# A two-layer hybrid attention block: balanced column halves, later row scaling, a later gate transposition, and one gated product behind a weight split

## The chip, the cores and the metric

The kernel runs on one core of a Trainium2 chip. The metric is device time in microseconds (us) from launch to end, the median of several runs of the same program. Beside it there is one profiled execution, whose trace says when each instruction ran on each engine: PE is TensorE (matmuls; PEld are its weight loads), DVE is VectorE, ACT is ScalarE, POOL is GpSimd, SP is the engine whose queue issues all DMAs here.

## The reference, cut to what matters

512 latent tokens `x` and 256 context tokens `ctx`, model width 1024, go through two layers. Everything is float32.

```python
for i in range(2):
    mod_x = silu(c) @ w_ada[i] + b_ada[i]            # six rows of 1024: sh1, sc1, g1, sh2, sc2, g2
    mod_c = silu(c_ctx) @ w_ada[i] + b_ada[i]        # the same for the context
    hx, hc = x * (1 + sc1) + sh1, ctx * (1 + csc1) + csh1
    # layer 0: windowed attention, 16 heads of 64; layer 1: differential attention, 8 pairs of heads
    ax, ac = mixer_i(hx, hc)                         # with its output projection
    x = layer_norm(alpha * x + g1 * ax)
    x = layer_norm(alpha * x + g2 * (square(relu((x * (1 + sc2) + sh2) @ w1[i])) @ w2[i]))
    if i == 0:                                       # the context takes part in layer 0's MLP too
        ctx = layer_norm(alpha * ctx + cg1 * ac)
        ctx = layer_norm(alpha * ctx + cg2 * mlp(ctx))
return x
```

So layer 0 works on 768 tokens, layer 1's queries and MLP on 512. Layer 1's attention takes, for each of 8 heads, two softmaxes over 768 keys, and subtracts one from the other.

## The kernel before, in words

**Products in three parts.** Each float32 operand is split into a rounded high part (`w_h`, made by ACT as a cast) and the rest (`w_l`, made by DVE as a subtraction). `mm3` issues high*high, high*low and low*high, so each product is three matmuls (lines 318, 319, 320). `wsplit` issues the DMA of a weight piece into `w_raw`, the cast and the subtraction. There are three `w_raw` buffers (a fourth later) and four pairs `w_h`, `w_l`, so a DMA waits until DVE has finished with an older piece.

**Order of work.** PE's order is fixed by a planner in the program (`Flow`): jobs are Python generators that yield a condition, and the planner goes on with the first job whose condition holds in its own model of time. The orders of the other engines are made from it by the scheduler of the framework; each engine then works through its own queue in order, waiting on semaphores. `tc.add_manual_dep(..., ORDER)` puts one instruction behind another in a queue without a wait; `behind(fn, ins)` adds a real wait on another engine's instruction.

**MLP of layer 0** (`mlp` with `ntok` = 768). Four chunks of 1024 hidden units. In a chunk, for each of eight groups `ft` of 128 hidden units, `h_ps` (two banks of PSUM, 1024 columns) takes 24 matmuls over the first 512 tokens and 24 over the other 256 (in chunk 0 the first two groups go in slices of 256). ACT reads it with a relu, DVE or POOL squares, ACT and DVE split into `hid`. Then `y_ps` products with `hid` follow. In chunks 0 to 3 DVE also works off `ada_rows`: dot products that give `mods`, the modulation rows still missing, from transposed weights (`w_raw<-in_w_adaT`, two or four DVE operations a row block). When such a row is complete, `ada_gate` transposes it on PE (`gate_t`), ACT copies it (`gate_s`), SP stores it (`gate_d`), and it is later loaded again as a row over all partitions. Row (0, 5), layer 0's second gate, is used in chunk 2.

**Layer 1's attention.** For each head `proj1` computes `qkv_ps` for six token blocks; `post1` rotates and splits the result, and PE transposes it (`kT_ps` from `sk`, `qT_ps` from `sq`). `scores1` makes `s_ps` (queries by 768 keys) with two matmuls of 512 columns and two of 256, then DVE takes the minimum `nm` and ACT the exponential. Beside it `resid1` prepares the residual of the output in 16 steps on POOL: `rs_x * rs_g + rs_b`. Each fourth step loads new `rs_g` and `rs_b` by DMA, and DVE scales them by `alpha`; that scaling stands where the load is issued.

**Layer 1's output projection** (`tok_product` and `gated_add`). For each token block and half, PE ends a sum `y_ps` whose first parts were made earlier; DVE multiplies by the gate row `g1x` (`g_tmp`), adds into `acc`, and takes statistics. The last weight piece, `b_wo[1, 3]`, is loaded at the start of this stage; `xn_t` are the transpositions after the normalisation, `hx_v`, `hx1m` their results.

Of the kernel before, what the change touches and what calls it, by code (L numbers as in the profile page):

```python
# [216 lines left out]
def pool2(n):  # L217
    return n * 0.0022 + 0.12
# [16 lines left out]
def hybrid_block(ctx: ExitStack, tc: tile.TileContext, t: dict, out: bass.AP):  # L235
# [63 lines left out]
    def wsplit(src, n=1024, raw=None, hl=None, pool=False):  # L299
        if raw is None:  # L300
            raw = raw_tile()
        if hl is None:
            hl = [wpool.tile([P, 1024], F32R, name="w_" + x, tag="w" + x, bufs=NH) for x in "hl"] + [rwh.get(), rwh]
        raw, rg, rr = raw
        h, l, hg, hr = hl
        q = dma(n, [rg], out=raw[:, :n], in_=src)
        a = ac(n, [q, hg], nc.scalar.copy, out=h[:, :n], in_=raw[:, :n])
        kw = dict(out=l[:, :n], in0=raw[:, :n], in1=f(h)[:, :n], op=ALU.subtract)
        d = gp(pool2(n), [a], nc.gpsimd.tensor_tensor, **kw) if pool else dv(n, [a], nc.vector.tensor_tensor, **kw)
        d.ring = rr  # L310
        rel = Task()
        rel.ring = hr
        return Weight(h, l, d, rel)
# [128 lines left out]

    def ada_gate(l, m, dep):
        gd = dram.tile([2 - l, KT, P], F32, name=f"gate_d{l}{m}")
        yield from to_rows(mods[l][:, m] if l == 0 else mods[l][:, m, :, 0], gd, dep)
        gate_d[(l, m)] = gd.rearrange("s k p -> s (k p)")

# [106 lines left out]
    def gated_add(pool, give, acc, half, pt, p, gate, last, scale=1.0):  # L554
        cs_ = slice(half * 512, (half + 1) * 512)
        tm = pool.tile([P, 512], F32, name="g_tmp", tag="tmp", bufs=2)
        m = dv(512, [p], nc.vector.tensor_tensor, out=tm, in0=pt, in1=gate[:, cs_], op=ALU.mult)
        give(m)
        if scale != 1.0:
            return dv(512, [m], nc.vector.scalar_tensor_tensor, out=acc[:, cs_], in0=acc[:, cs_], scalar=scale, in1=tm,  # L560
                      op0=ALU.mult, op1=ALU.add)
        if last:
            return dv(512, [m], nc.vector.tensor_tensor, out=acc[:, cs_], in0=acc[:, cs_], in1=tm, op=ALU.add)
        return gp(pool2(512), [m], nc.gpsimd.tensor_tensor, out=acc[:, cs_], in0=acc[:, cs_], in1=tm, op=ALU.add)
# [76 lines left out]
    def mlp(l, hx, ready, apool, pool, ntok, acc, gates, done, extra, res, XR=0):  # L641
        ntb = ntok // P
        first = [slice(i, i + 256) for i in range(0, ntok, 256)]
        parts = [slice(0, 512)] + ([slice(512, ntok)] if ntok > 512 else [])
        fx = [pool.tile([P, D], F32, name="fx", tag="fx", bufs=ntb) for _ in range(ntb)]


# [16 lines left out]

        row_gates = gates
        for ch in range(4):
            hid = [apool.tile([P, 2, 2, ntok], F32R, name="hid", tag="A", bufs=4) for _ in range(4)]
            state = {}

            def post(ft, pt, slot, p):  # L670
                hd, fi = hid[ft // 2], ft % 2
                r = pool.tile([P, max(ntok, XR)], F32, name="relu", tag="xr", bufs=2)
                a = ac(ntok, [p], nc.scalar.activation, out=r[:, :ntok], in_=pt[:, :ntok], func=AF.Relu)
                if slot is not None:
                    sS.give(slot, a)
                if ch:
                    a = gp(pool2(ntok), [a], nc.gpsimd.tensor_tensor, out=r[:, :ntok], in0=r[:, :ntok],
                           in1=r[:, :ntok], op=ALU.mult)
                else:
                    a = dv(ntok, [a], nc.vector.tensor_tensor, out=r[:, :ntok], in0=r[:, :ntok], in1=r[:, :ntok],  # L680
                           op=ALU.mult)
                split(ntok, a, r[:, :ntok], hd[:, fi, 0], hd[:, fi, 1])

            n0 = 0 if ch else 2 if ntok > 512 else 4
            order = [(ft, sl) for sl in first for ft in range(n0)] + [(ft, sl) for ft in range(n0, 8) for sl in parts]
            for n, (ft, sl) in enumerate(order):
                if ch == 0:
                    yield lambda: [ready[b] for b in range(sl.start // P, sl.stop // P)]
                if sl.start == 0:
                    odd = n0 == 4 and ft in (1, 3)  # L690
                    if not odd:
                        yield sS.ok
                        state["ps"] = psS("h_ps"), sS.take()
                    pt, slot = state["ps"]
                    state[ft] = (wsplit(t["w1"][l, ch * 8 + ft], pool=ch == 0 and ft in WP[l]), pt[:, 512:1024] if odd else pt,
                                 None if n0 == 4 and ft in (0, 2) else slot)
                w, pt, slot = state[ft]
                yield w.t
                for k in range(KT):
                    c_ = slice(k * P, (k + 1) * P)  # L700
                    mm3(pt[:, sl], w.h[:, c_], w.l[:, c_], hxs(hx, k, 0, sl), hxs(hx, k, 1, sl), k == 0, k == KT - 1)
                    if k % 4 == 3:
                        p = fl.pe(12 * mm(sl.stop - sl.start))
                        if k == 3:
                            yield
                if sl.stop == ntok:
                    fl.finish(w.rel)
                    post(ft, pt, slot, p)
                if extra is not None and (4 < n < 16 if ch == 0 else ft < 6 and sl.start == 0):
                    next(extra, None)  # L710
                yield
            if ch == 2:
                gates = yield from row_gates()
            yield from tok_product(pool, hid, lambda half: [wsplit(t["w2"][l, ch, half, u]) for u in range(4)],
                                   [(h_, tb) for h_ in range(2) for tb in range(ntb)], acc, gates,
                                   done if ch == 3 else None, extra=extra, sink=sum_up(ch, gates) if ch < 3 else None)
# [461 lines left out]
    with tc.tile_pool(name="attn1", bufs=1, reuse_waits="tile") as pool:  # L1178
# [104 lines left out]
        def resid1():  # L1283
            def load(n):
                i, tb = n // NXB, n % NXB
                c = slice(i * 256, i * 256 + 256)
                if tb == 0:
                    gb[:] = [pool.tile([P, 256], F32, name="rs_" + n_, tag="rs_" + n_, bufs=1) for n_ in "gb"]
                    for k in range(2):
                        dma(256, [], out=gb[k], in_=lnrow[0, 2 + k:3 + k][:, c].broadcast_to([P, 256]))  # L1290
                        dv(128, [], nc.vector.tensor_scalar, out=gb[k], in0=gb[k], scalar1=ALPHA, scalar2=None,
                           op0=ALU.mult)
                x = pool.tile([P, 256], F32, name="rs_x", tag="rs_x", bufs=3)
                return x, dma(256, [], out=x, in_=x_spill[tb][:, c]), x_res[tb][:, c], list(gb)

# [2 lines left out]
            for n in range(4 * NXB):  # L1298
                after = yield
                x, q, dst, (g, b) = nxt  # L1300
                d = gp(pool2(256), [q], behind(nc.gpsimd.tensor_tensor, after), out=x, in0=x, in1=g, op=ALU.mult)
                d = gp(pool2(256), [d], nc.gpsimd.tensor_tensor, out=x, in0=x, in1=b, op=ALU.add)
                if old:
# [8 lines left out]
        def scores1(hd_, R):  # L1312
            kS, qTt = R["kS"], R["qT"]
            yield lambda: R["ready"]
            for qb in range(4):
                em = []
                for tt in range(2):
# [1 line left out]
                    ei = eS1.take()  # L1319
                    sp = psS("s_ps")  # L1320
                    slot = sS.take()
                    for c0, c1 in ((0, 512), (512, TOK)):
                        for hl in range(2):
                            nc.tensor.matmul(out=sp[:, c0:c1], lhsT=qTt[:, tt, hl, qb * P:(qb + 1) * P],  # L1324
                                             rhs=kS[:, tt, c0:c1], start=(hl == 0), stop=(hl == 1))
                    p = fl.pe(2 * mm(512) + 2 * mm(256))
                    nm = small.tile([P, 1], F32, name="nm", tag="nm")
                    d = dv(TOK, [p], nc.vector.tensor_reduce, out=nm, in_=sp[:, 0:TOK], axis=AX.X, op=ALU.min)
                    e = pool.tile([P, TOK], F32, name="e1", tag="e", bufs=EB1)
                    if tt == 0:  # L1330
                        sm = st["s0"][hd_ // NG][:, qb, hd_ % NG:hd_ % NG + 1]
                    else:
                        sm = small.tile([P, 1], F32, name="sm", tag="sm")
                    a = ac(TOK + 200, [d], nc.scalar.activation, out=e, in_=sp[:, 0:TOK], func=AF.Exp, scale=-1.0,
                           bias=nm, accum_out=sm)
                    sS.give(slot, a)
                    em.append((e, sm, ei, a))
                    yield
# [172 lines left out]
    with tc.tile_pool(name="mlp1", bufs=1, reuse_waits="tile") as pool:  # L1511
# [5 lines left out]
        gx = bcast_load(pool, gate_d[(1, 2)][0:1], "g1x")  # L1517
        queue["behind"] = queue["last"]
        st2["W1"].append(wsplit(t["b_wo"][1, 3], hl=hl + [None, None]))
        lb = bcast_load(pool, lnrow[1, 1:2], "l1b")  # L1520
        scale_inplace(lb, ALPHA)
        A, B = affine(1, 0, 1, 1, 3, 4, "m1", 1)
# [106 lines left out]
```

## Time and profile before

| | us |
|---|---|
| median of 3 runs | 1710.75 (1710.18 to 1711.88) |
| the profiled execution's own time | 1715.99 |
| span of its trace, first to last instruction | 1714.2 |

| engine | busy, us | share |
|---|---|---|
| PE | 1634.3 | 95% |
| DVE | 957.7 | 56% |
| ACT | 658.1 | 38% |
| POOL | 345.9 | 20% |

PE's mean granted clock was 0.985. A matmul's record lasts longer than its share of PE, since matmuls overlap: the pace is read from start to start. A row of the timeline gives start, length, engine, line, operation, and in brackets how long the engine had been idle and what ended that.

### The profile page before, as it was taken

The numbers are of one execution on the slowest core, as the hardware profiler recorded it, in microseconds if no ns is written. First come the engines' busy times: TensorE is split into PE (matmuls) and PEld (weight loads), VectorE is DVE, ScalarE is ACT, GpSimd is POOL, SyncE is SP. The second block draws the span as 40 slices with busy tenths as digits, with TensorE's granted clock in tenths as the row PEclk, the third lists the DMA queues.
The fourth block names the chain that finished last, engine by engine and source line by source line (L and its number), as shares of the span: only waits on it lengthen the run. The fifth ranks groups of instructions, "written<-read, shape, count | busy, mean of one in ns | idle before, by whom it ended". The sixth has DMA issues, their size and how long they took to land.

```text
span 1714.2 us, 23438 instructions
## 1 busy us (share of the span) xinstructions
PE 1634.3 (95%) x9129; PEld 1359.1 (79%) x9129; DVE 957.7 (56%) x1811; ACT 658.1 (38%) x1281; POOL 345.9 (20%) x314
## 2 busy tenths in 40 slices
PE   6899899999899999999999999999989799999998
PEld 4787567788778878878878998999877788888886
DVE  3665677676764644445346767777655553233336
ACT  3455555462212302302315555555542533223230
POOL 1233444200001201243220122220100001103422
PEclk9999999999999999999999999999999899999999
DMA  9110441243443434324222222211132214232321
GB/s 361 40 50 32 148 171 52 84 169 112 159 147 111 148 111 141 111 91 156 81 81 102 63 68 66 72 44 37 47 111 99 99 62 134 74 121 76 111 86 50
DMA packets 57240, 174.78 MB, mean 102 GB/s; under 512 B 7144, under 2 KB 13096, under 8 KB 57128
## 3 DMA queue, kind: packets, MB, share of 16 engines
q1 hardware_dynamic: 57128, 173.27, 29.9%
q8 instruction: 72, 1.18, 0.3%
q14 instruction: 40, 0.33, 0.1%
HBM read 165.35 MB, written 7.90 MB: 101 GB/s over the span
## 4 chain that ended last, share of the span: by engine, by line
PE 75%; DVE 9%; issue 5%; ACT 4%; POOL 3%; DMA 3%; SPq 0%; POOLq 0%; DVEq 0%; ACTq 0%
PE y_ps L320 10%; PE y_ps L319 10%; PE y_ps L318 10%; PE h_ps L318 8%; PE h_ps L319 8%; PE h_ps L320 8%; PE o_ps L1014 2%; PE qkv_ps L318 2%; PE s_ps L1324 2%; PE qkv_ps L319 2%; PE qkv_ps L320 2%; DVE e L260 2%; DVE w_l L260 2%; PE pT_ps L1028 2%; ACT w_h L264 1%
## 5 line engine op out<-in xcount | busy, mean ns | idle before, releaser
L264 ACT CAST w_h<-w_raw 128x1024 fp32r<-128x1024 f32 (+1 forms) x185 | 186.5, 1014 | 425.5 <-PE y_ps L320 214.1
L260 DVE TENSOR_TENSOR w_l<-w_raw,w_h 128x1024 fp32r<-128x1024 f32 (+1 forms) x185 | 221.9, 1209 | 223.5 <-ACT w_h L264 223.4
L319 PE MATMUL y_ps<-w_l,hid 128*128 128x512 f32 x640 | 253.0, 395 | 2.2 <-DVE w_l L260 2.2
L320 PE MATMUL y_ps<-w_h,hid 128*128 128x512 f32 x640 | 252.9, 395 | 0.6 <-DVE hid L260 0.6
L318 PE MATMUL y_ps<-w_h,hid 128*128 128x512 f32 x640 | 253.0, 395 | 0.0
L268 POOL TENSOR_TENSOR relu<-relu 128x768 f32<-128x768 f32 (+1 forms) x48 | 81.5, 1697 | 613.9 <-ACT relu L264 613.9
L320 PE MATMUL h_ps<-hx0m,w_l 128*128 128x256 f32 (+1 forms) x528 | 176.2, 334 | 0.9 <-DVE w_l L260 0.9
L318 PE MATMUL h_ps<-hx0m,w_h 128*128 128x256 f32 (+1 forms) x528 | 176.7, 335 | 0.0
L319 PE MATMUL h_ps<-hx0m,w_h 128*128 128x256 f32 (+1 forms) x528 | 176.0, 333 | 0.0
L319 PEld LDWEIGHTS y_ps<-w_l,hid 128*128 128x128 f32 x640 | 120.4, 188 | 31.7 <-DVE w_l L260 3.9
L320 PEld LDWEIGHTS y_ps<-w_h,hid 128*128 128x128 f32 x640 | 120.4, 188 | 30.1 <-DVE hid L260 1.9
L318 PEld LDWEIGHTS y_ps<-w_h,hid 128*128 128x128 f32 x640 | 120.4, 188 | 28.4
L318 PE MATMUL qkv_ps<-w_h,hx 128*128 128x384 f32 (+1 forms) x384 | 128.2, 334 | 0.2
L319 PE MATMUL qkv_ps<-w_l,hx 128*128 128x384 f32 (+1 forms) x384 | 123.7, 322 | 0.8 <-DVE w_l L260 0.8
L320 PE MATMUL qkv_ps<-w_h,hx 128*128 128x384 f32 (+1 forms) x384 | 123.4, 321 | 0.0
L268 POOL TENSOR_TENSOR e<-e,sm 128x512 f32<-128x512 f32 (+2 forms) x96 | 95.4, 1010 | 127.6 <-DVE sm L260 107.1
L318 PE MATMUL h_ps<-hx1m,w_h 128*128 128x512 f32 (+1 forms) x288 | 108.1, 375 | 3.5 <-ACT relu L264 3.5
L320 PEld LDWEIGHTS h_ps<-hx0m,w_l 128*128 128x128 f32 x528 | 99.7, 189 | 12.9 <-DVE w_l L260 1.7
L318 PEld LDWEIGHTS h_ps<-hx0m,w_h 128*128 128x128 f32 x528 | 99.7, 189 | 11.4 <-ACT w_h L264 0.2
L319 PEld LDWEIGHTS h_ps<-hx0m,w_h 128*128 128x128 f32 x528 | 99.7, 189 | 11.3
L319 PE MATMUL h_ps<-hx1m,w_h 128*128 128x512 f32 (+1 forms) x288 | 107.6, 374 | 0.0
L320 PE MATMUL h_ps<-hx1m,w_l 128*128 128x512 f32 (+1 forms) x288 | 107.5, 373 | 0.0
(225 smaller groups left out, 3124.1 us busy)
## 6 DMA issues: line engine op xcount, KB each, us to landing
w_raw<-in_w SPq DMA_DIRECT2D x128, 512.0 KB, 3.5
w_raw<-in_w_adaT SPq DMA_DIRECT2D x56, 512.0 KB, 3.5
w_raw<-in_w_ada SPq DMA_DIRECT2D x24, 512.0 KB, 3.9
w_raw<-in_b_w SPq DMA_DIRECT2D x32, 384.0 KB, 3.4
raw<-in_w_ada SPq DMA_DIRECT2D x16, 512.0 KB, 9.6
w_raw<-in_a_wq SPq DMA_DIRECT2D x8, 512.0 KB, 7.1
w_raw<-in_a_wo SPq DMA_DIRECT2D x8, 512.0 KB, 3.6
w_raw<-in_b_wo SPq DMA_DIRECT2D x8, 512.0 KB, 4.4
```

The costliest lines, as they stand in the source:

```text
L260: fn(**kw)
L264: fn(**kw)
L268: fn(**kw)
L318: nc.tensor.matmul(out=o, lhsT=lh, rhs=rh, start=start, stop=False)
L319: nc.tensor.matmul(out=o, lhsT=lh, rhs=rl, start=False, stop=False)
L320: last["pe"] = nc.tensor.matmul(out=o, lhsT=ll, rhs=rh, start=False, stop=stop)
L1014: nc.tensor.matmul(out=po[odd * HD:odd * HD + HD, 0:256], lhsT=vv[:, kb, kvh], rhs=pt_[:, odd * 256:odd * 256 + 256], start=(i == 0), stop ...
L1028: nc.tensor.transpose(out=pp[:, c * P:(c + 1) * P], in_=es[j][:, i * P:(i + 1) * P], identity=ident)
L1324: nc.tensor.matmul(out=sp[:, c0:c1], lhsT=qTt[:, tt, hl, qb * P:(qb + 1) * P], rhs=kS[:, tt, c0:c1], start=(hl == 0), stop=(hl == 1))
```

## The change

Six edits, joined:

1. In layer 0's MLP the 768 tokens go in halves of 384 and 384, not 512 and 256. The second half is written at column 512 of `h_ps`, so each half lies in one bank; the relu reads the two stretches as a two-dimensional pattern.
2. The scores of layer 1 go in the same way, two matmuls of 384 columns for each half of the keys; the minimum and the exponential read the two stretches.
3. The transposition of row (0, 5) (`gate_t`) waits in the planner until chunk 1 of layer 0's MLP begins.
4. The scaling of `rs_g` and `rs_b` moves from the place of the load to the step that first uses them, with a wait on the PE transposition `kT_ps` of that step.
5. In DVE's queue the first gated product of layer 1's output projection stands behind the subtraction of the last weight piece.
6. `wsplit` and `gated_add` keep the instruction for that (no instruction of their own).

```diff
@@ wsplit @@
+            last["split"] = nc.vector.tensor_tensor(**kw)
+            d = fl.op("D", dve(n), [a])
@@ ada_gate @@
+        if (l, m) == (0, 5):
+            yield lambda: YES if "second" in st2 else NO
@@ gated_add @@
-        m = dv(512, [p], nc.vector.tensor_tensor, out=tm, in0=pt, in1=gate[:, cs_], op=ALU.mult)
+        i = nc.vector.tensor_tensor(out=tm, in0=pt, in1=gate[:, cs_], op=ALU.mult)
+        if queue.get("split"):
+            tc.add_manual_dep(i.ins, queue.pop("split"), ORDER, reason="queue order")
+        m = fl.op("D", dve(512), [p])
@@ mlp @@
-        parts = [slice(0, 512)] + ([slice(512, ntok)] if ntok > 512 else [])
+        parts = [slice(0, 512)] if ntok <= 512 else [slice(0, ntok // 2), slice(ntok // 2, ntok)]
+            if l == 0 and ch == 1:
+                st2["second"] = True
-                a = ac(ntok, [p], nc.scalar.activation, out=r[:, :ntok], in_=pt[:, :ntok], func=AF.Relu)
+                ro, ri = r[:, :ntok], pt[:, :ntok]
+                if ntok > 512 and ft >= n0:
+                    ro = ro.rearrange("p (b t) -> p b t", b=2)
+                    ri = pt.rearrange("p (b t) -> p b t", b=2)[:, :, 0:ntok // 2]
+                a = ac(ntok, [p], nc.scalar.activation, out=ro, in_=ri, func=AF.Relu)
+                    po = sl if ft < n0 or sl.start == 0 else slice(512, 512 + sl.stop - sl.start)
+                    mm3(pt[:, po], w.h[:, c_], w.l[:, c_], hxs(hx, k, 0, sl), hxs(hx, k, 1, sl), k == 0, k == KT - 1)
@@ resid1 @@
-                        dv(128, [], nc.vector.tensor_scalar, out=gb[k], in0=gb[k], scalar1=ALPHA, ...)
+                for y in (g, b) if n % NXB == 0 else ():
+                    dv(128, [], behind(nc.vector.tensor_scalar, after), out=y, in0=y, scalar1=ALPHA, ...)
@@ scores1 @@
-                    for c0, c1 in ((0, 512), (512, TOK)):
+                    for c in range(2):
                         for hl in range(2):
+                            nc.tensor.matmul(out=sp[:, c * 512:c * 512 + 384], lhsT=qTt[:, tt, hl, qb * P:(qb + 1) * P],
+                                             rhs=kS[:, tt, c * 384:c * 384 + 384], start=(hl == 0), stop=(hl == 1))
+                    sv = sp.rearrange("p (b t) -> p b t", b=2)[:, :, 0:384]
+                    d = dv(TOK, [p], nc.vector.tensor_reduce, out=nm, in_=sv, axis=AX.XY, op=ALU.min)
+                    a = ac(TOK + 200, [d], nc.scalar.activation, out=e.rearrange("p (b t) -> p b t", b=2),
+                           in_=sv, func=AF.Exp, scale=-1.0, bias=nm, accum_out=sm)
@@ before layer 1's output projection @@
         st2["W1"].append(wsplit(t["b_wo"][1, 3], hl=hl + [None, None]))
+        queue["split"] = last["split"].ins.name
```

What moves in the queues. First PE, in chunk 0 of layer 0's MLP, where `gate_t` stood between two groups of hidden units (`h_ps`, from activations `hx0m` and weights):

```order
L320 MATMUL h_ps<-hx0m,w_l 128x256
L435 MATMUL gate_t<-identr,mods_81 16x128
L318 MATMUL h_ps<-hx0m,w_h 128x512
L319 MATMUL h_ps<-hx0m,w_h 128x512
L320 MATMUL h_ps<-hx0m,w_l 128x512
```

Now it stands 384 matmuls later, behind the last product of chunk 0 (`y_ps`) and ahead of the first of chunk 1:

```order
L324 MATMUL y_ps<-w_h,hid 128x512
L439 MATMUL gate_t<-identr,mods_81 16x128
L322 MATMUL h_ps<-hx0m,w_h 128x384
L323 MATMUL h_ps<-hx0m,w_h 128x384
L324 MATMUL h_ps<-hx0m,w_l 128x384
```

On SP the store of that row moves with it, behind 22 more weight loads, and the two loads of the row behind eight more; in DVE's queue some dot products of `ada_rows` go behind `w_l` subtractions, and none is added.

Second DVE, in layer 1's attention, at the end of a head (the two last blocks of a head are context tokens, whose `sk` is split straight from `qkv_ps`; `rms_sb` belongs to the head before). Before:

```order
L260 TENSOR_TENSOR vt_8449<-qkv_ps,vt_8449 128x128
L260 TENSOR_SCALAR rs_g<-rs_g 128x256
L260 COPY rms_sb<-rms_ps 128x128
L260 TENSOR_SCALAR rs_b<-rs_b 128x256
L260 TENSOR_TENSOR sk<-qkv_ps,sk 128x2x64
L260 TENSOR_TENSOR w_l<-w_raw,w_h 128x768 x3
```

Now:

```order
L260 TENSOR_TENSOR vt_8449<-qkv_ps,vt_8449 128x128
L260 COPY rms_sb<-rms_ps 128x128
L260 TENSOR_TENSOR sk<-qkv_ps,sk 128x2x64
L312 TENSOR_TENSOR w_l<-w_raw,w_h 128x768 x3
```

The two scalings left this place; they stand in the next head behind two minima `nm`. The same happens in the heads after it, four times in all. In the third of these heads the planner also interleaves PE's `pT_ps`, `o_ps`, `kT_ps`, `qT_ps` and `qkv_ps` in another order; the rest of PE's order is as before.

Third DVE, at the start of layer 1's output projection. Before:

```order
L260 TENSOR_TENSOR oT_8245<-oraw,oT_8245 128x512 x2
L260 TENSOR_TENSOR g_tmp<-y_ps,g1x 128x512
L260 TENSOR_TENSOR acc_12405<-acc_12405,g_tmp 128x512
L260 BN_STATS bn<-acc_12405 128x6
L260 TENSOR_TENSOR w_l<-w_raw,w_h 128x1024
L260 TENSOR_SCALAR l1b<-l1b 128x1024
L260 TENSOR_TENSOR g_tmp<-y_ps,g1x 128x512
```

Now:

```order
L260 TENSOR_TENSOR oT_8245<-oraw,oT_8245 128x512 x2
L312 TENSOR_TENSOR w_l<-w_raw,w_h 128x1024
L260 TENSOR_SCALAR l1b<-l1b 128x1024
L563 TENSOR_TENSOR g_tmp<-y_ps,g1x 128x512
L260 TENSOR_TENSOR acc_12405<-acc_12405,g_tmp 128x512
L260 BN_STATS bn<-acc_12405 128x6
L563 TENSOR_TENSOR g_tmp<-y_ps,g1x 128x512
```

The subtraction and the scaling of `l1b` moved ahead of three instructions.

More of the change, by code (lines that the diff above doesn't have):

```diff
@@ L308, in wsplit @@
         kw = dict(out=l[:, :n], in0=raw[:, :n], in1=f(h)[:, :n], op=ALU.subtract)
-        d = gp(pool2(n), [a], nc.gpsimd.tensor_tensor, **kw) if pool else dv(n, [a], nc.vector.tensor_tensor, **kw)
+        if pool:
+            d = gp(pool2(n), [a], nc.gpsimd.tensor_tensor, **kw)
+        else:
+            last["split"] = nc.vector.tensor_tensor(**kw)
+            d = fl.op("D", dve(n), [a])
         d.ring = rr
@@ L700, in mlp @@
                     c_ = slice(k * P, (k + 1) * P)
-                    mm3(pt[:, sl], w.h[:, c_], w.l[:, c_], hxs(hx, k, 0, sl), hxs(hx, k, 1, sl), k == 0, k == KT - 1)
+                    po = sl if ft < n0 or sl.start == 0 else slice(512, 512 + sl.stop - sl.start)
+                    mm3(pt[:, po], w.h[:, c_], w.l[:, c_], hxs(hx, k, 0, sl), hxs(hx, k, 1, sl), k == 0, k == KT - 1)
                     if k % 4 == 3:
@@ L1290, in load @@
                         dma(256, [], out=gb[k], in_=lnrow[0, 2 + k:3 + k][:, c].broadcast_to([P, 256]))
-                        dv(128, [], nc.vector.tensor_scalar, out=gb[k], in0=gb[k], scalar1=ALPHA, scalar2=None,
-                           op0=ALU.mult)
                 x = pool.tile([P, 256], F32, name="rs_x", tag="rs_x", bufs=3)
@@ L1300, in resid1 @@
                 x, q, dst, (g, b) = nxt
+                for y in (g, b) if n % NXB == 0 else ():
+                    dv(128, [], behind(nc.vector.tensor_scalar, after), out=y, in0=y, scalar1=ALPHA, scalar2=None,
+                       op0=ALU.mult)
                 d = gp(pool2(256), [q], behind(nc.gpsimd.tensor_tensor, after), out=x, in0=x, in1=g, op=ALU.mult)
@@ L1321, in scores1 @@
                     slot = sS.take()
-                    for c0, c1 in ((0, 512), (512, TOK)):
+                    for c in range(2):
                         for hl in range(2):
-                            nc.tensor.matmul(out=sp[:, c0:c1], lhsT=qTt[:, tt, hl, qb * P:(qb + 1) * P],
-                                             rhs=kS[:, tt, c0:c1], start=(hl == 0), stop=(hl == 1))
-                    p = fl.pe(2 * mm(512) + 2 * mm(256))
+                            nc.tensor.matmul(out=sp[:, c * 512:c * 512 + 384], lhsT=qTt[:, tt, hl, qb * P:(qb + 1) * P],
+                                             rhs=kS[:, tt, c * 384:c * 384 + 384], start=(hl == 0), stop=(hl == 1))
+                    sv = sp.rearrange("p (b t) -> p b t", b=2)[:, :, 0:384]
+                    p = fl.pe(4 * mm(384))
                     nm = small.tile([P, 1], F32, name="nm", tag="nm")
-                    d = dv(TOK, [p], nc.vector.tensor_reduce, out=nm, in_=sp[:, 0:TOK], axis=AX.X, op=ALU.min)
+                    d = dv(TOK, [p], nc.vector.tensor_reduce, out=nm, in_=sv, axis=AX.XY, op=ALU.min)
                     e = pool.tile([P, TOK], F32, name="e1", tag="e", bufs=EB1)
@@ L1333, in scores1 @@
                         sm = small.tile([P, 1], F32, name="sm", tag="sm")
-                    a = ac(TOK + 200, [d], nc.scalar.activation, out=e, in_=sp[:, 0:TOK], func=AF.Exp, scale=-1.0,
-                           bias=nm, accum_out=sm)
+                    a = ac(TOK + 200, [d], nc.scalar.activation, out=e.rearrange("p (b t) -> p b t", b=2),
+                           in_=sv, func=AF.Exp, scale=-1.0, bias=nm, accum_out=sm)
                     sS.give(slot, a)
```

## The prediction, as put on record before the run

> **What bounds the kernel now.** I read the page first: which engine is busy.
>
> ```profile
> PE 1634.3 (95%) x9129; PEld 1359.1 (79%) x9129; DVE 957.7 (56%) x1811; ACT 658.1 (38%) x1281; POOL 345.9 (20%) x314
> ```
>
> PE bounds the kernel. A change can take time out of its pace or out of its waits. So next I read whom PE waits for, longest first (total, times, longest):
>
> ```profile
> PE kT_ps L1229 <- DVE sk L260: 8.5, 6, 2.3
> ...
> PE y_ps L319 <- DVE w_l L260: 5.3, 5, 3.1
> ...
> PE gate_t L435 <- DVE mods L260: 4.9, 1, 4.9
> ```
>
> Three of the longest are places that the diff touches: DVE's queue at the ends of heads, the last weight piece, and the transposition of the gate row. The granted clock (the number after the five engines; instructions in brackets) says what stands behind each wait:
>
> ```profile
> 433.90:438.80 4.90, 4.89 (x12) 3.87 (x13) 3.56 (x5) 1.30 (x2) 0.00 (x0) 0.50 0.66 213
> 1001.60:1005.40 3.80, 3.79 (x18) 3.80 (x19) 2.76 (x4) 1.56 (x4) 0.00 (x0) 0.55 0.64 205
> 1310.40:1313.70 3.30, 0.18 (x1) 0.00 (x0) 3.23 (x5) 0.00 (x0) 0.00 (x0) 0.83 0.00 0
> 1313.70:1319.40 5.70, 5.70 (x13) 4.46 (x14) 2.54 (x4) 0.00 (x0) 0.00 (x0) 0.50 0.77 265
> ```
>
> After each of the three waits PE runs at half clock for some microseconds, and in the third row the clock falls inside the wait. So a wait costs more than its idle time.
>
> **A. The gate transposition** (edit 3). PE's and DVE's rows:
>
> ```profile
> 428.78 0.28 PE L320 MATMUL h_ps<-hx0m,w_l 128*128 128x256 f32 x1
> 433.91 0.38 PE L435 MATMUL gate_t<-identr,mods 128*16 128x128 f32 x1 [4.85 <-DVE mods L260]
> 434.01 0.76 PE L318 MATMUL h_ps<-hx0m,w_h 128*128 128x512 f32 x1
> 439.06 0.40 PE L318 MATMUL h_ps<-hx0m,w_h 128*128 128x512 f32 x1
> 428.51 1.23 DVE L260 TENSOR_TENSOR w_l<-w_raw,w_h 128x1024 fp32r<-128x1024 f32 x1 [1.28 <-ACT w_h L264]
> 437.56 1.23 DVE L260 TENSOR_TENSOR w_l<-w_raw,w_h 128x1024 fp32r<-128x1024 f32 x1 [1.29 <-ACT w_h L264]
> ```
>
> The idle time is 4.85. From 434.01 to 439.06 twelve matmuls of 512 columns took 5.05; at 0.233 each (below) they take 2.80, so half clock cost 2.25. Together 7.1. The transposition itself stays, with operands long ready. What is late next is `w_l`: without the wait PE would want the first of the two pieces at 428.9 + 0.47 (it serves the third matmul) and have it at 429.74, and the second (8.4 later) at about 438.2, to have it at 438.79. That is 0.4 + 0.6 = 1.0 which the stall hid. A = 6.1, between 4.5 (PE also waits in the new place, by a wait like the 1.03 under C, and a little more) and 7.1 (`w_l` comes earlier).
>
> The store and the loads of the row now stand ahead of weight loads on SP. At 520.3, where chunk 0's products end, those loads have several pieces of lead; I cost this at nothing, and it is a rival below.
>
> **B. First end of a head** (edit 4). Here DVE waits for two DMAs ahead of `sk` (the first row is the page's, with the median time to landing):
>
> ```profile
> w_raw<-in_b_w SPq DMA_DIRECT2D x32, 384.0 KB, 3.4
> 1001.61 0.33 PE L1229 MATMUL kT_ps<-identr,sk 128*128 128x128 f32 x2 [2.31 <-DVE sk L260]
> 999.56 0.29 DVE L260 TENSOR_SCALAR rs_g<-rs_g 128x256 f32<-128x256 f32 x1 [1.60 <-DMA rs_g<-in_lnrow]
> 1000.97 0.29 DVE L260 TENSOR_SCALAR rs_b<-rs_b 128x256 f32<-128x256 f32 x1 [0.92 <-DMA rs_b<-in_lnrow]
> 1002.36 7.32 SPq L275 DMA_DIRECT2D w_raw<-in_b_w  x4
> 1008.36 0.96 DVE L260 TENSOR_TENSOR w_l<-w_raw,w_h 128x768 fp32r<-128x768 f32 x1 [2.46 <-ACT w_h L264]
> 1009.54 0.34 PE L318 MATMUL qkv_ps<-w_h,hx 128*128 128x384 f32 x1
> ```
>
> Without the two waits PE gains 2.3, and the half clock behind them (1001.60 to 1005.40 at 0.55: 3.8 x 0.45 = 1.7): 4.0. But the head's fourth weight piece then ends last: its DMA goes out at 1002.36, DVE ends its split at 1009.32, and PE wants it at 1009.54, now 4.0 earlier. The DMA waits in SP's queue behind loads of `rs_x` until about 1001.6, so the chain gains 0.75 at least, and PE 0.9 with the 0.2 that it had to spare. The transfer took some 5 here (to the cast of 0.87 ahead of 1008.36), against 3.4 at the median; with that, 1.7 more, at most 2.8. I take 2.0, nearer to the usual transfer.
>
> **C. Second and third ends.** The second end against the fourth, where nothing is loaded any more for `rs_x` (rows of 1124.09 and 1128.88):
>
> ```profile
> 1039.89 0.43 PE L1420 MATMUL rms_ps<-osq,c_selT 128*32 128x128 f32 x8
> 1046.32 0.60 PE L1449 MATMUL rmsB<-identr,rr 128*2 128x128 f32 x4 [0.54 <-POOL rr L268]
> 1124.09 0.43 PE L1420 MATMUL rms_ps<-osq,c_selT 128*32 128x128 f32 x8
> 1128.88 0.60 PE L1449 MATMUL rmsB<-identr,rr 128*2 128x128 f32 x4 [1.03 <-POOL rr L268]
> 1083.90 0.29 DVE L260 TENSOR_SCALAR rs_g<-rs_g 128x256 f32<-128x256 f32 x1 [3.69 <-DMA rs_g<-in_lnrow]
> ```
>
> 6.43 against 4.79: the scalings cost 1.6 there, and POOL's `rr` ends last in both. The third DVE wait, 3.69, is the longest, but PE's six waits for `sk` were 8.5 together and at most 2.3, and the largest of them were elsewhere: it is hidden but for some tenths, and I take 0.2. C = 1.8, between 1.0 and 2.2. In their new places the scalings stand behind minima that end after `kT_ps` in all four heads, so I cost their added waits at nothing; if one came early, DVE would hold the next exponential's input for some tenths. PE's new order in the third head: 0, between 1.0 lost and 1.0 gained, as waits in the ends of heads are of that size.
>
> **D. The gated product behind the last split** (edit 5).
>
> ```profile
> 1301.93 1.04 ACT L264 CAST w_h<-w_raw 128x1024 fp32r<-128x1024 f32 x1
> 1310.38 0.69 DVE L260 TENSOR_TENSOR g_tmp<-y_ps,g1x 128x512 f32<-128x512 f32 x1 [7.63 <-PE y_ps L320]
> 1312.44 1.21 DVE L260 TENSOR_TENSOR w_l<-w_raw,w_h 128x1024 fp32r<-128x1024 f32 x1
> 1310.18 0.40 PE L318 MATMUL y_ps<-w_h,oT 128*128 128x512 f32 x1
> 1313.70 0.80 PE L319 MATMUL y_ps<-w_l,oT 128*128 128x512 f32 x1 [3.13 <-DVE w_l L260]
> 1318.80 0.69 DVE L260 TENSOR_TENSOR g_tmp<-y_ps,g1x 128x512 f32<-128x512 f32 x1 [1.14 <-PE y_ps L320]
> 1330.33 0.69 DVE L260 TENSOR_TENSOR g_tmp<-y_ps,g1x 128x512 f32<-128x512 f32 x1 [0.30 <-PE y_ps L320]
> ```
>
> The piece was ready at 1302.97, and DVE sat idle 7.63 in front of the gated product, with the split behind it. Now the split runs in that idle time. PE alone gains 3.52 - 0.23 (1310.18 to 1313.70, less one matmul) and, over the 13 matmuls to 1319.40 (the last clock row), 5.70 - 3.03 = 2.7: 6.0. Then DVE ends last: from 1318.80 on it was busy until 0.30 before 1330.33, 11.2 for the third to the eighth gated product. With its first products back to back (two steps of 0.7 each behind 1312.4) the third starts at 1313.9 and the eighth at 1325.1, 5.2 earlier, when PE has just ended its part. The normalisation, `xn_t` and the MLP follow that. D = 5.2, between 3.3 (the clock falls anyway) and 6.0.
>
> [...]
>
> **E. Halves of 384** (edits 1, 2).
>
> ```profile
> 402.01 0.39 PE L318 MATMUL h_ps<-hx0m,w_h 128*128 128x512 f32 x1
> 407.60 0.28 PE L318 MATMUL h_ps<-hx0m,w_h 128*128 128x256 f32 x1
> 399.20 0.28 PE L318 MATMUL h_ps<-hx0m,w_h 128*128 128x256 f32 x1
> 970.04 0.34 PE L318 MATMUL qkv_ps<-w_h,hx 128*128 128x384 f32 x1
> 973.18 0.40 PE L1324 MATMUL s_ps<-kS,qT 128*128 128x512 f32 x1
> ```
>
> 24 matmuls of 512 columns (402.01 to 407.60) take 5.59, 0.233 each; 24 of 256 (399.20 to 402.01) take 2.81, 0.117 each; 18 of 384 take 3.14, 0.174 each. A group costs 8.40 now and 48 x 0.1744 = 8.37 then. 6 groups in chunk 0 and 24 in the others: 0.9 gained. The scores: 64 times 0.003, 0.2. The relu reads as many columns as before, in two stretches, beside matmuls. E = 1.1; as some runs of 384 go by 0.002 slower than this one, the lower end is -2.4.
>
> **The sum.** 6.1 + 2.0 + 1.8 + 5.2 + 1.1 = 16.2. The profiled execution took 1715.99, with 1.8 around its span; it would take 1699.8. It lies 5.2 above the median of the runs, 1710.75; the terms are waits which these runs have too, so I take them from the median: 1694.5.
>
> **Rivals.**
> 1. The half-clock stretches stay, since they come with these stages and not with these waits. Against it speaks that in all three places the clock fell at the wait. Only idle time goes: 4.85 - 1.0 in A, 0.9 in B, 1.8 in C, 3.3 in D, 1.1 in E: 11, so 1700. Chance 0.12. [...]
> 2. SP's queue: the moved store waits for ACT's copy, the load behind it for the store, and weight pieces of chunk 1 for both. One late piece costs a DMA's way and a stretch of half clock, as in A, 7: the gain shrinks to 9, 1702. Against it: PE reaches that point 6 earlier while the weights are several pieces ahead. Chance 0.07.
> 3. Slower: a matmul of 384 columns over `hx0m` into `h_ps` costs more than over `hx` into `qkv_ps`, since the row that I price it by streams weights, not activations. There are 30 x 48 = 1440 of them. The other terms gain 15.3; from 0.185 each the kernel is no faster, from 0.187 it is slower by over 0.2%. At 0.233, the price of a whole bank, it would be 1780. Nothing in the profile speaks for it; chance 0.03.
> 4. PE's waits move instead of going (the next weight piece, POOL's `rr`, DVE's normalisation), and what is left can't be told from no change, 0.2% being about what a measurement of this kernel can tell: 1709. Chance 0.04.
>
> **Numbers.** My forecast has the rest, 0.74, with a range of its own from 1689 (all upper ends: 7.1 + 2.8 + 2.2 + 6.0 + 1.1, the third head's order 1.0, and the 4.0 of B in full, together 21.4) to 1699. The whole range reaches to 1702, for rivals 1 and 2. Faster 0.93 (the forecast and rivals 1 and 2), same 0.04, slower 0.03.
>
> **What would show it.** The trace afterwards should have no wait at `gate_t`, no half clock near 430 and at the output projection, and none of the waits of DVE for `rs_g`; a short wait for `w_l` in the first head's end; 48 matmuls in 8.37. It is wrong if `h_ps` matmuls start more than 0.18 apart, if ACT waits for `in_w` early in chunk 1, or if the clock falls at new places.

## The result and the profile after

| | before | all changes |
|---|---|---|
| median, us | 1710.75 (1709.49 to 1711.88, 5 runs) | 1699.93 (1699.34 to 1701.91, 5 runs) |
| ratio | | 0.9939 [0.9925, 0.9954] |
| profiled execution, us | 1715.99, span 1714.2 | 1701.91, span 1700.1 |
| mean granted clock in it | 0.985 | 0.988 |

The kernel is faster by 10.8 us, where 16.2 were forecast; between the two profiled executions the difference is 14.1. Two more samples of the same kernel, among the experiments, gave ratios of 0.9938 and 0.9931.

The engines after the change, from the page:

```profile
PE 1629.0 (96%) x9129; PEld 1392.8 (82%) x9129; DVE 956.8 (56%) x1811; ACT 658.2 (39%) x1281; POOL 347.0 (20%) x314
```

PE is busy for 5.3 us less, and still bounds the kernel. PE's waits (total, times, longest):

```profile
PE kT_ps L1246 <- DVE sk L260: 7.9, 6, 2.3
...
PE y_ps L323 <- DVE w_l L312: 1.7, 2, 1.3
...
PE qkv_ps L323 <- DVE w_l L312: 0.8, 2, 0.6
```

The wait at `gate_t` (4.9) is gone from the list, and `y_ps` waits 1.7 for `w_l` instead of 5.3. The waits of `qkv_ps` for `w_l` are 0.8 together as before, but the longest has moved from the third head's end (1093.59) to the first's, where the prediction expected one. The waits for `sk` are hardly shorter in sum, 7.9 instead of 8.5: the 2.31 of the first head's end is gone, and one of 1.71 in the third head is new. The longest that is left, 2.32, is that of a later head, which no edit touches.

PE's timeline shows the places one after the other: the gate row's transposition, 48 matmuls of 384 columns (counted from 518.98; the 49th starts at 527.30), and the first head's end:

```profile
512.91 0.40 PE L324 MATMUL y_ps<-w_h,hid 128*128 128x512 f32 x1
513.15 0.27 PE L439 MATMUL gate_t<-identr,mods 128*16 128x128 f32 x1
513.17 0.42 PE L322 MATMUL h_ps<-hx0m,w_h 128*128 128x384 f32 x1
...
518.98 0.34 PE L322 MATMUL h_ps<-hx0m,w_h 128*128 128x384 f32 x1
...
527.30 0.34 PE L322 MATMUL h_ps<-hx0m,w_h 128*128 128x384 f32 x1
...
997.57 0.45 PE L322 MATMUL qkv_ps<-w_h,hx 128*128 128x384 f32 x1 [0.33 <-ACT w_h L264]
998.56 0.45 PE L323 MATMUL qkv_ps<-w_l,hx 128*128 128x384 f32 x1 [0.55 <-DVE w_l L312]
```

The transposition runs without a wait, and chunk 1 begins at 513.17 (before: at 520.5). The 48 matmuls take 8.32. In the first head's end the fourth weight piece now ends last, with waits of 0.33 and 0.55 in place of the 2.31 for `sk`.

In the output projection DVE's queue now has the split where it was meant to be, ahead of the idle time:

```profile
1295.30 1.22 DVE L312 TENSOR_TENSOR w_l<-w_raw,w_h 128x1024 fp32r<-128x1024 f32 x1 [0.26 <-ACT w_h L264]
1296.44 0.69 DVE L260 TENSOR_SCALAR l1b<-l1b 128x1024 f32<-128x1024 f32 x1
1302.67 0.69 DVE L563 TENSOR_TENSOR g_tmp<-y_ps,g1x 128x512 f32<-128x512 f32 x1 [5.55 <-PE y_ps L324]
```

Last, stretches of the timeline with PE's granted clock behind the five engines: the first head's end, a place in the third head, the output projection, and the end of a later head.

```profile
998.40:1002.20 3.80, 3.64 (x21) 3.63 (x22) 3.37 (x10) 2.04 (x5) 0.29 (x1) 1.00 0.34 103
1065.80:1069.20 3.40, 2.80 (x14) 2.40 (x13) 2.40 (x6) 1.44 (x3) 0.58 (x1) 0.50 0.28 81
...
1298.00:1304.00 6.00, 6.00 (x27) 4.84 (x27) 1.29 (x2) 0.00 (x0) 0.00 (x0) 1.00 0.65 245
1202.30:1212.60 10.30, 10.30 (x31) 9.02 (x31) 5.48 (x7) 4.01 (x8) 0.00 (x0) 0.50 0.32 118
```

The half clock of the first head and the one behind the split in the output projection are gone (both rows at 1.00). A stretch at 1065.8 is new (0.50), and the one near 1203, at a place that the change doesn't touch, is 10.2 long instead of 6.8. This last point turned out to matter for the whole case: the program had not changed there.

### The profile page after: what moved, and what is told of

The parts are those of the page before. It is cut to its first block, busy times and chain, and to the rows that moved or that the text cites. A ratio compares the mean times of both kernels' runs of the same rounds, so it can differ in the third digit from the quotient of the medians.

```text
span 1700.1 us, 23451 instructions
## 1 busy us (share of the span) xinstructions
PE 1629.0 (96%) x9129; PEld 1392.8 (82%) x9129; DVE 956.8 (56%) x1811; ACT 658.2 (39%) x1281; POOL 347.0 (20%) x314
## 4 chain that ended last, share of the span: by engine, by line
PE 76%; DVE 10%; ACT 4%; issue 3%; DMA 3%; POOL 3%; SPq 0%; DVEq 0%; POOLq 0%; ACTq 0%
PE y_ps L324 10%; PE y_ps L322 10%; PE y_ps L323 10%; PE h_ps L322 8%; PE h_ps L323 8%; PE h_ps L324 8%; PE o_ps L1031 2%; PE qkv_ps L322 2%; PE qkv_ps L323 2%; PE s_ps L1342 2%; PE qkv_ps L324 2%; PE pT_ps L1045 2%; DVE w_l L312 2%; DVE e L260 2%; PE o_ps L1380 1%
## 5 line engine op out<-in xcount | busy, mean ns | idle before, releaser
L312 DVE TENSOR_TENSOR w_l<-w_raw,w_h 128x1024 fp32r<-128x1024 f32 (+1 forms) x185 | 220.3, 1202 | 221.0 <-ACT w_h L264 218.6
L324 PE MATMUL h_ps<-hx0m,w_l 128*128 128x384 f32 (+1 forms) x528 | 175.4, 332 | 1.3 <-DVE w_l L312 1.3
L322 PE MATMUL h_ps<-hx0m,w_h 128*128 128x384 f32 (+1 forms) x528 | 175.4, 332 | 0.0
L323 PE MATMUL h_ps<-hx0m,w_h 128*128 128x384 f32 (+1 forms) x528 | 175.1, 332 | 0.0
```

The costliest lines, as they stand in the source:

```text
L312: last["split"] = nc.vector.tensor_tensor(**kw)
L322: nc.tensor.matmul(out=o, lhsT=lh, rhs=rh, start=start, stop=False)
L323: nc.tensor.matmul(out=o, lhsT=lh, rhs=rl, start=False, stop=False)
L324: last["pe"] = nc.tensor.matmul(out=o, lhsT=ll, rhs=rh, start=False, stop=stop)
```

## The experiments

All ran with five rounds beside the kernel before. Differences below are of medians unless they are called differences of stages in a profile. The first four had no run of all of the changes beside them; they are set against the 1699.93 above.

**The scalings' new place, the old plan.** The scalings stand where the change puts them, but the planner is told of them at the old place, so PE's order in the heads is that of before:

```diff
@@ resid1, load @@
+                        fl.op("D", dve(128), [])
@@ resid1, step @@
-                    dv(128, [], behind(nc.vector.tensor_scalar, after), out=y, in0=y, scalar1=ALPHA, ...)
+                    behind(nc.vector.tensor_scalar, after)(out=y, in0=y, scalar1=ALPHA, ...)
```

> The changed kernel, with the planner told of the two scalings at their old place (the instructions stay at the new one): PE's order in layer 1's attention is that of before. Theory 1 (the third head's new order cost 2.8 us: a wait of 1.7 for sk and half clock behind it): 1697.1 us, ratio to before 0.992, no wait over 0.5 us for sk in the third head. Rival (that wait only took the place of others; the third DMA wait of DVE, 3.69 us, was what the head had to lose): 1699.9 us, as the changed kernel, with another wait in the third head.

1699.11 us, ratio 0.9936 [0.9924, 0.9949]. By the milestones of the two profiles its third head was about 2.5 shorter, by the median the whole was not to be told from all of the changes.

**The gate back** (edit 3 undone).

```diff
-        if (l, m) == (0, 5):
-            yield lambda: YES if "second" in st2 else NO
```

> The changed kernel without the later gate transposition. Theory 1 (the stall costs its idle time and half clock behind it, in every run): 1706.5 us (6.6 more than the changed kernel), a wait of 4.9 us at gate_t and half clock behind it. Rival (in most runs the clock does not fall, so that a run loses only the idle time less 1.0): 1703.8 us (3.9 more).

1705.46, ratio 0.9975 [0.9964, 0.9986]: 5.5 slower than all of the changes (6.2 by the ratios), between the 6.6 of the first theory and the 3.9 of the rival, and near the 6.1 at which the prediction priced edit 3.

**The split back** (edit 5 undone).

```diff
-        queue["split"] = last["split"].ins.name
```

> The changed kernel without the order between the first gated product and the last split. Theory 1 (idle time and half clock, DVE last): 1705.7 us (5.8 more than the changed kernel), a wait of 3.1 us for w_l in the output projection. Rival (only the idle time counts in most runs): 1703.2 us (3.3 more).

1699.36, ratio 0.9938 [0.9924, 0.9952]: as fast as all of the changes. Neither theory had said so. Its profile has the wait of 3.1 again, but no half clock behind it (1.00 from 1293.0 to 1306.8).

**The scalings back** (edit 4 undone, with PE's order of before in the heads).

```diff
@@ resid1, load @@
+                        dv(128, [], nc.vector.tensor_scalar, out=gb[k], in0=gb[k], scalar1=ALPHA, ...)
@@ resid1, step @@
-                for y in (g, b) if n % NXB == 0 else ():
-                    dv(128, [], behind(nc.vector.tensor_scalar, after), out=y, in0=y, scalar1=ALPHA, ...)
```

> The changed kernel with the scalings back at the load, and so with PE's old order in the third head. Theory 1 (the move gained 1.6 at the first and 1.6 at the second end of a head, and lost 2.8 in the third): 1700.3 us, the same as the changed kernel within what can be measured. Rival (the move gained what its waits showed, 4 in all, and the third head's wait was there in another place): 1703.9 us.

1698.68, ratio 0.9935 [0.9921, 0.995]: edit 4, priced at 3.8 with its two terms, is worth nothing that the medians show, as the first theory had it.

Two terms were now open, the split's and the scalings'. The second set had all of the changes beside it on the same chip.

**All of the changes again**, the same program.

> All of the changes once more, as a second sample beside the kernels below and a second profile. If the half-clock stretches fall where a program's waits put them, this profile has them at the same seven places and the same 42.3 us of half clock as the first, within one stretch of 3.4, and a span near 1700.1. If their places also depend on something that runs by itself, so that a stretch comes or not from one execution to the next, the total differs by two stretches or more (25.2 to 52.6 us were seen over the profiles so far), and the span minus half of the total stays near 1700.1 - 21.2 = 1678.9 within 1.5. Median 1699.9 by both, 1698.5 to 1701.5.

1700.59, ratio 0.9938 [0.9922, 0.9954]. By its records of the clock the total of half clock was 42.8 us, near the first profile's 42.5, and the span less half of it 1676.3, 2.6 below the 1678.9 that the expectation gave within 1.5. But the two records don't begin at the same time. This one starts at 11.8 and so counts a stretch from 15.2 to 22.0; that of the first profile starts at 24.7 with the turn to full clock, and the matmuls of 256 columns ahead of it start 0.213 apart (0.117 at full clock), so PE was slow there too. Without that stretch the total here is 36.0, 6.5 or about two stretches less than in the first profile, and the span less half of it 1679.7, as the second theory had it: the stretch at 1065.8 is gone, the one near 1203 is 6.8 instead of 10.2, and one at 66.4 is new. So the same program has other stretches in another execution.

**The split alone**: the kernel before with the lines of edits 5 and 6 only.

> The kernel before with one change only: the queue order of the split. Theory of the prediction (the wait of 3.1 us and the half clock behind it, 5.2 in all): 5.2 us less than before, ratio 0.997. Theory 'the wait alone' (idle 3.1 goes, at most 1.9 of later waits come in its place, the half clock comes as often as before): 1.2 to 3.1 us less, ratio 0.998 to 0.999. Theory 'nothing' (VectorE has the same work ahead of the normalisation, and what TensorE doesn't wait for at the split it waits for at the transposes): 0 within 0.7, and the wait at xn_t grows by what the wait for the split loses.

1707.83 against 1711.61, ratio 0.9982 [0.997, 0.9994]: 3.1 gained by the ratio, 1 to 5 by its interval: the upper end of what the wait alone would give, with the prediction's 5.2 at the far end. It is worth something; the first experiment on it had misled.

**The old plan again.**

> The scalings where the change puts them, but TensorE's order in the heads of before: the same kernel as the run with the old plan, beside all of the changes on one chip. Theory 'the third head's new order costs what the profile showed': 2.8 us less than all of the changes (1.7 of it the wait for kT behind sk, the rest half clock). Rival 'only the wait counts, the half clock there was chance': 1 to 1.7 us less. Rival 'nothing in the median': within 0.7 of all of the changes.

1698.63, ratio 0.9923 [0.9906, 0.9939], 2.0 less than all of the changes beside it, with intervals that overlap. It has the lowest ratio of all, but only the stages below tell it from all of the changes.

**The MLP's halves back** (512 and 256 columns; the main line of the edit, the relu's view and the column offset go back with it).

```diff
-        parts = [slice(0, 512)] if ntok <= 512 else [slice(0, ntok // 2), slice(ntok // 2, ntok)]
+        parts = [slice(0, 512)] + ([slice(512, ntok)] if ntok > 512 else [])
```

> All of the changes but the MLP's halves: its matmuls are 512 and 256 columns wide again. By the spacings in the profiles (2 x 174.7 = 349.4 ns for a pair of 384s, 233.3 + 117.4 = 350.7 for 512 and 256) 1.3 ns a pair over 768 pairs: 1.0 us more than all of the changes. By the milestones of the profiles, up to 2.0 us more. Rival (width costs nothing, the 1.3 to 2 were clock): 0 within 0.5. TensorE's half clock is the same within the spread by all.

1699.80, ratio 0.9937 [0.9921, 0.9952]: 0.8 under all of the changes beside it, the wrong sign for a price of 1, and well inside the intervals.

**The split back again**, on the chip of the next three.

> All of the changes but the queue order of the split, as the run with the split back, now beside all of the changes on one chip. In that run the median was that of all of the changes although its profile showed the wait of 3.1 us at the split; the half clock came in 25.3 us instead of 42.3. Theory 'the wait counts, the half clock falls by the phase of its grid' (all starts of a profile lie on multiples of 3.413 us from each other, to within 0.1): the wait of 3.1 is there again, the half clock has another total, and the median stands 1 to 3.5 us over all of the changes. Theory of the prediction: 5.2 over. Rival 'with the other edits the order of the split is worth nothing, what is saved there is lost at once': within 1.0 again.

1705.19, ratio 0.9969 [0.9958, 0.998]: now 6.7 over all of the changes beside it, more than any of the three theories gave. The same program had stood at 0.9938 [0.9924, 0.9952]. The profile of this run has the half clock at the split (0.50 from 1301.3 to 1308.1).

**All of the changes a third time.**

> All of the changes a third time, for the comparison on this chip and a third profile: ratio 0.9938 within 0.001. Theory of the grid: the starts of the half clock again lie 3.413 us or whole multiples of it apart, from another offset than in the first two profiles, and at least one stretch of 3.4 us is gone, new or of another length. Rival (the stretches are the program's own): the same seven as in the first profile.

1698.47, ratio 0.9931 [0.9918, 0.9945]; a third set of stretches, 32.4 us together (mean granted clock 0.991, against 0.988 in the first profile).

**The gate alone**: the kernel before with edit 3 only.

> The kernel before with one change only: the gate row's transposes wait for the second chunk. By the prediction 6.1 us less than before (4.5 to 7.1): the wait of 4.9 us and half of its half clock. By the run with the gate back (5.5 to 6.2 more than all of the changes): 5.5 to 6.2 less. Rival 'the wait alone': 4.9 less or a little under. With the split alone (3.1 less) it should then make up 8 to 9 of the 10.6 us that all of the changes give.

1703.21 against 1709.67, ratio 0.9961 [0.9945, 0.9976]: 6.5 gained (4 to 9 by the interval of the ratio, so that the median alone doesn't rule out the rival's 4.9). With the split alone (3.1 by its ratio) this makes 9.6 of the 10.8.

**The scores back** (512 and 256 columns in layer 1's scores; the main line of the edit, the views of the minimum and the exponential go back with it).

```diff
-                    for c in range(2):
+                    for c0, c1 in ((0, 512), (512, TOK)):
```

> All of the changes but the scores' halves: 512 and 256 columns again in the score matmuls. By the spacings 2 x 174.7 against 233.3 + 117.4 ns: 1.3 ns a pair, some 0.1 to 0.2 us more than all of the changes, not to be told from nothing. A rival by the row reduction and the exponential, which now read two pieces in one instruction: if that were dearer, this run would be up to 1 us faster than all of the changes, with shorter waits of s_ps for nm.

1698.79, ratio 0.9938 [0.9922, 0.9954]: 0.3 over all of the changes beside it, not to be told from nothing.

### Stage by stage, over all of the profiles

Medians of 5 to 12 runs could not separate terms of 1 to 3 us. But the fourteen profiles (before, after and the twelve runs) are fourteen executions, and each stage exists in them with and without its edit. Each length runs between starts of PE instructions; "head n" is the first `rms_ps` of that head's end, in order of time.

| stage | without its edit | with it | gained |
|---|---|---|---|
| first `xn_t` of layer 0's MLP to chunk 1 (edit 3) | 167.9, 168.0, 167.6 | 160.6 to 163.2, mean 161.8 (11) | 6.0 |
| chunk 1 to head 1 (edit 1) | 476.2 to 476.8, mean 476.4 (4) | 474.1 to 477.3, mean 475.6 (10) | 0.8 |
| head 1 to head 2 (edit 4) | 42.2 to 42.6, mean 42.4 (4) | 40.5 to 41.3, mean 40.8 (10) | 1.6 |
| head 2 to head 3 (edit 4, old plan) | 43.6 to 43.8, mean 43.7 (4) | 42.5, 42.6 | 1.2 |
| the same, with the changed plan | | 43.8 to 45.0, mean 44.3 (8) | -0.6 |
| head 3 to head 4 (edit 4) | 40.1 to 41.3, mean 40.6 (4) | 40.3 to 40.6, mean 40.4 (10) | 0.2 |
| head 8 to the first `xn_t` of layer 1's MLP (edit 5) | 40.4, 40.5, 37.8, 37.7 | 34.6 to 34.7 (10) | 5.8 or 3.1, mean 4.5 |

The gains, with the changed plan, make 6.0 + 0.8 + 1.6 - 0.6 + 0.2 + 4.5 = 12.5. The interval of the ratio gives 8 to 13 us for the whole, so this closes, though near its end; what is left, 1.7 to the medians, is within what single executions differ by.

### Why the split's wait cost 5.8 in two executions and 3.1 in two

All four have the same wait of 3.1 for `w_l`. Here are the rows of the timeline around it, one line for each 3.4 us, laid out from the half-clock stretches of that execution (the shortest records of half clock in the profiles before and after are 3.413 long); the second number of a row is PE's busy time, the number behind the five engines its granted clock. Before:

```profile
1309.20:1312.60 3.40, 1.38 (x6) 0.76 (x5) 2.15 (x4) 0.00 (x0) 0.00 (x0) 1.00 0.00 0
1312.60:1316.00 3.40, 2.30 (x5) 1.82 (x6) 1.66 (x2) 0.00 (x0) 0.00 (x0) 0.50 0.38 102
```

The split back, first run:

```profile
1293.00:1296.50 3.50, 1.84 (x8) 1.14 (x7) 1.79 (x3) 0.00 (x0) 0.00 (x0) 1.00 0.00 0
1296.50:1299.90 3.40, 1.93 (x8) 1.61 (x9) 2.49 (x4) 0.00 (x0) 0.00 (x0) 1.00 0.29 73
1299.90:1303.30 3.40, 3.40 (x16) 2.74 (x15) 3.37 (x8) 0.00 (x0) 0.00 (x0) 1.00 0.96 360
```

The split back again:

```profile
1297.90:1301.30 3.40, 1.16 (x5) 0.59 (x4) 2.37 (x4) 0.00 (x0) 0.00 (x0) 1.00 0.00 0
1301.30:1304.70 3.40, 2.51 (x6) 2.03 (x7) 1.44 (x2) 0.00 (x0) 0.00 (x0) 0.50 0.42 124
```

The gate alone, where the split's order is that of before:

```profile
1296.70:1300.10 3.40, 2.01 (x9) 1.30 (x7) 1.52 (x3) 0.00 (x0) 0.00 (x0) 1.00 0.00 0
1300.10:1303.50 3.40, 1.66 (x7) 1.40 (x8) 2.49 (x4) 0.00 (x0) 0.00 (x0) 1.00 0.21 46
```

In the two executions where most of the wait falls into one row (idle 2.02 and 2.24 of 3.40), the next row is at half clock (0.50). In the two where the wait is cut in two (idle 1.66 and 1.47; 1.39 and 1.74), the clock stays full (1.00). The program alone doesn't set where the stretches lie: all of the changes had one at 1065.8 in its first profile and none there in its second. So edit 5 saves 3.1 in all four and 2.7 more in two. That the place of the wait is the cause of the 2.7 was not shown: it is an estimate from these four executions, and in a later head it is otherwise (last section), where a wait that is cut in two is followed by half clock all the same. Nor does the 2.7 account for the 5.8 between the medians of the two runs with the split back. Their profiles are 5.9 apart in span (1695.2 and 1701.1): 2.7 in this stage, 1.9 ahead of the first `xn_t` of layer 0's MLP, where the second has a stretch of half clock at 253 that the first lacks, 1.4 between heads 4 and 8, where its stretch near 1202 is 6.8 instead of 3.4, and the rest in parts of both signs, at most 1.2 each. Why the medians of the two sets differ by as much isn't shown, since their other executions have no profile.

### What the third head's new order costs

After the change, the timeline of PE in the third head, and then that of DVE beside it:

```profile
1061.34 0.29 PE L1246 MATMUL kT_ps<-identr,sk 128*128 128x128 f32 x2
1061.46 0.95 PE L1380 MATMUL o_ps<-pT,vt 128*128 128x256 f32 x6
1062.25 0.45 PE L1261 MATMUL qT_ps<-identr,sq 128*128 128x128 f32 x4
1064.41 0.34 PE L1246 MATMUL kT_ps<-identr,sk 128*128 128x128 f32 x2 [1.71 <-DVE sk L260]
```

```profile
1061.76 0.70 DVE L260 SCALAR_TENSOR_TENSOR nl<-s,nlam,rc 128x1 f32<-128x1 f32 x1
1062.49 1.57 DVE L260 SCALAR_TENSOR_TENSOR e<-e,nl,e 128x768 f32<-128x768 f32 x1
1063.99 0.28 DVE L260 TENSOR_TENSOR sk<-rope,sk 128x128 fp32r<-128x128 f32 x1
```

With the old plan (the first of its two runs), PE at the same place:

```profile
1061.47 0.29 PE L1246 MATMUL kT_ps<-identr,sk 128*128 128x128 f32 x2
1061.59 0.50 PE L1261 MATMUL qT_ps<-identr,sq 128*128 128x128 f32 x4
1061.94 0.41 PE L322 MATMUL qkv_ps<-w_h,hx 128*128 128x384 f32 x1
...
1063.93 0.34 PE L324 MATMUL qkv_ps<-w_h,hx 128*128 128x384 f32 x1
1064.10 0.29 PE L1246 MATMUL kT_ps<-identr,sk 128*128 128x128 f32 x2
```

In the old plan a run of `qkv_ps` matmuls stands between one `kT_ps` and the next, and the second doesn't wait. In the changed plan only six `o_ps` matmuls and the `qT_ps` stand there. DVE is in the combination of the two softmaxes (1.57) with `sk` behind it, and PE waits 1.71, as it does within 0.01 in all eight profiles with the changed plan. In the profile after, a stretch of half clock follows (0.50 from 1065.80 to 1069.20). The stage takes 44.7 to 45.0 in three of the eight, this one among them, else 43.8 to 44.4.

## Why the prediction was right, and where it was not

- **Time and direction.** 1699.93 lies in the range of 1689 to 1702 and is 5.4 above the forecast of 1694.5; it lies 0.9 beyond the 1699 that the forecast gave itself, in the part that was kept for rivals 1 and 2. Neither of them is what happened, so that the time lies in the range is in part luck.
- **A, 6.1.** Right: 6.0 by the stages, 6.5 by the gate alone, 5.5 by the gate back. The wait of 4.85 in the profile before had half clock behind it (4.90 at 0.50), and the two other profiles that have the wait took as long for the stage (168.0 and 167.6, against 167.9).
- **B, 2.0.** 1.6 by the stages, for the reason given: the first head's fourth weight piece ends last now, with waits of 0.33 and 0.55. The upper end of 2.8 doesn't follow from its terms: 0.75 + 0.2 + 1.7 = 2.65.
- **C, 1.8.** 1.2 and 0.2 by the stages, if PE's order stays.
- **"PE's new order in the third head: 0."** This step failed. It was bounded by 1.0 on either side; it cost 44.3 - 42.6 = 1.7 in the mean, so that what C gained there was lost. The prediction took the change in order for a shuffle, and didn't ask what DVE would be doing when the second `sk` is wanted. The stretch of half clock at 1065.8 is the sign "if the clock falls at new places" that the prediction had named.
- **D, 5.2.** Right in its mechanism: the split went into the idle time, and DVE's tail follows (34.6 to 34.7 in all ten). The half clock, 2.7, was counted as certain because the one profile of before had it; two of four have it. With it the stage gained 5.8, without it 3.1; in the mean of the four 4.5.
- **E, 1.1.** 0.8 by the MLP's stage and not seen in the medians. The third rival, that a 384 into `h_ps` costs more, fell: 48 take 8.32.
- **"So I take them from the median."** The sum was made on a profiled execution of 1715.99 and subtracted from 1710.75. Its half-clock stretches were part of the terms, but that execution had more of them than usual: its mean granted clock was 0.985, where 51 later runs of the same kernel had 0.984 to 0.990 with a mean of 0.988, and none of them took over 1714.5. Against its own time the sum gave 1699.8, and the profiled execution after took 1701.91.
- **Rival 1, half clock stays, 1700.** The number came out, the mechanism didn't: it gave A only 3.85, and A's stage gained 6.0. What is true of it is D's half clock in some executions.
- **Rival 2, SP's queue.** PE waits for nothing in chunk 1. ACT does wait for `in_w` there, by up to 4.0, which the prediction had named as a sign of being wrong; but it waited by up to 5.1 at the same place before, so the sign could not have told.
- **Rival 4**, waits that move: true of 1.7 in the third head.

Of the 5.4 that the forecast was off, the third head accounts for 1.7, D's half clock for 0.7 in the mean, B, C and E for 0.4 + 0.4 + 0.3 and A for 0.1. That is 3.6; the other 1.8 is not settled.

## What to carry to other kernels

Price an idle wait by its idle time, and its half clock only by the share of executions that have it (two of four at the split here): several profiles of the same program show that share, and the length of a stage over many profiles settles what medians of a few runs can't. When a change makes a planner write out another order, go through the new order and look for the instruction whose producer is behind a long one on its engine; don't price it at nothing because it only reorders. Two experiments on one edit that differ by more than their intervals (0.9938 and 0.9969 for one program here) are a sign that something beside the program varies.

## What the runs showed of the hardware

The waits of PE named above, and the half clock that came with them:

| wait of PE, profile | idle, us | half clock |
|---|---|---|
| `gate_t` for `mods`, before | 4.85 | 6.83 from 431.96, inside the wait |
| `kT_ps` for `sk`, first head's end, before | 2.31 | 3.41 from 1001.99, behind it |
| `y_ps` for `w_l`, the split, before | 3.13 | 6.83 from 1312.60, inside the wait |
| the same, the split back again | 3.1 | 6.8 from 1301.3 |
| the same, the split back (first run) and the gate alone | 3.1 | none, 1.00 |
| `kT_ps` for `sk`, third head, after | 1.71 | 3.41 from 1065.76, behind it |
| `kT_ps` for `sk`, a later head, before | 2.32 | 6.83 from 1213.62, behind it |
| the same, after | 2.32 | 10.24 from 1202.29, behind it |

In the profiles before and after, the records of half clock (ten and seven) start whole multiples of 3.413 us apart, to within 0.002, with an offset of 1.88 from the span's start before and 0.80 after. But for the last one of each profile they are 3.41, 6.83 or 10.24 long.

In the profile before, spans of 3.413 counted from these starts cut the 2.32 of the later head in two (idle 1.05 and 1.27 between matmul records, whose ends are modelled, so this is rough). Half clock came after the second part all the same, while the split's 3.1, cut in two, left the clock full twice. So the idle time of a wait is not all that decides, and what else does is open.
